# One more of eight depthwise-convolution channel blocks on the tensor engine, and another order of the layer norm's partial sums

## The chip, the cores and the metric

The kernel runs on one core of a Trainium2 chip. The metric is the device time of one execution in microseconds, as the median of several runs. Engines are called by their short names: PE is the tensor engine, DVE the vector engine, ACT ScalarE, POOL GpSimd, SP the engine that here only issues DMAs.

## The reference

Two decoder layers over 512 positions and 1024 channels, all in float32. Layer 0 mixes with an mLSTM, layer 1 with the convolution module below; each is followed by a gated MLP. The change lies in the convolution module alone:

```
C_KERNEL = 31

def conformer_conv_mixer(x, w_in, b_in, dw_w, dw_b, ln_g, ln_b, w_out, b_out):
    a = x @ w_in + b_in
    u = a[..., :D_MODEL] * jax.nn.sigmoid(a[..., D_MODEL:])
    u = causal_dwconv(u, dw_w, dw_b)
    u = jax.nn.silu(layernorm(u, ln_g, ln_b))
    return u @ w_out + b_out
```

The depthwise convolution has 31 taps for each channel. The layer norm takes mean and variance over all 1024 channels of a position.

## The kernel before, in words

Activations lie with channels on the 128 partitions and the 512 positions along the free axis, so 1024 channels are 8 blocks of 128 x 512. A matmul in float32 precision is made of three passes over operands that are split into a high and a low part (`mm3`): a weight unit of 128 x 1024 is loaded by SP, cast to its high part by ACT (line 151), and the rest is subtracted on DVE (line 152). Units come through rings: 4 raw, 3 high and 3 low. `next_unit` asks for the casts two units ahead.

The convolution stage runs over the 8 blocks j in order. `glu(j)` multiplies two weight units into two PSUM banks (24 matmuls for each unit), scales both on DVE, takes the sigmoid on ACT, and writes `u` on DVE. What then happens to `u` depends on the block's list:

- Blocks in `DVE_CH` and most taps of block 0 are convolved by taps on DVE: `dve_tap` (line 765), one fused multiply-add of 128 x 512 for each tap, into a PSUM bank.
- Block 1 (`POOL_CH`) and 13 taps of block 0 go by pairs: ACT makes the product of one tap (line 752, a ring of 4 buffers), POOL adds it (line 754). Block 0's two accumulators are joined later.
- Blocks in `PE_CH` go to PE. `shuffle` has ACT issue four DMAs that rearrange `u` into `us` (positions of four phases). `toeplitz` has POOL build block-diagonal weights `toe` of four groups (line 777). `conv_pe` multiplies them in two halves (line 804); each half is copied out by ACT (line 809) and goes back into channel order through two DMAs, one issued by ACT and one by SP (line 812). `us`, `toe` and the result each have a ring of two.

Taps wait in two lists, and `background(nv, ng)` takes so many from each. `PLAN` says what follows block j's own work: key 5 and 6 for the convolutions of blocks 3 and 5, key 14 and 15 (j + 8) for sums behind those of blocks 6 and 7.

`shift` takes the first PE block (`FIRST`), computes its mean over the 128 channels with a pair of matmuls (`col_mean`, lines 229 and 230, operands `ch` by ACT and `cl` by DVE), and uses this, `kb`, as an offset for all blocks. `stats(j, e)` subtracts it, squares on ACT, and adds block and square to `s1` and `s2` on engine e (POOL or DVE). The last PE block and the last DVE block are not added there; they go to the sums as parts of their own. `row_sums` (line 242) multiplies 128 x 128 pieces by two columns of 1/1024, and line 912 forms the mean over channels in all partitions. `warm(n, p)` runs n small float32 matmuls (two passes each, line 101) whose result nobody reads. Behind the sums come variance, a power on POOL, the broadcast of its rows, and for each block normalisation, activation and split on DVE and ACT, which feed the output projection (`out_proj`).

The order on each engine is made by a scheduler at build time: among the instructions that its own model holds ready, it takes the one that comes first in the program. `tc.issue_after(x)` holds an instruction behind x on its engine. On the chip each engine then works in that order.

Of the kernel before, what the change touches and what calls it, by code (L numbers as in the profile page):

```python
# [45 lines left out]
def hybrid_trunk(ctx, tc, x_in, par_in, tph_in, wg_in, wv_in, wqk_in, wo_in, mout_in, cin_in,  # L46
                 cout_in, up_in, down_in, out):
    nc = tc.nc
    V, A, G, PE = nc.vector, nc.scalar, nc.gpsimd, nc.tensor
# [12 lines left out]
    def nm(s):  # L62
        uid[0] += 1
        return f"{s}_{uid[0]}"

    def bank():
        return psum.tile([P, T], F32, tag="mm", name=nm("mm"))

    def small():
        return psms.tile([P, T], F32, tag="ms", name=nm("ms"))  # L70
# [5 lines left out]
    def pcol(name, i):  # L76
        o = _COLS[name] + i
        return par[:, o : o + 1]
# [8 lines left out]
    invd = const.tile([P, P], F32, name="invd")  # L87
# [8 lines left out]
    def warm(n, after=None):  # L96

        ps = bank()
        for _ in range(n):
            with tc.issue_after(after.ins) if after is not None else nullcontext():  # L100
                after = PE.matmul(ps[:, :P], ones, ones, start=True, stop=True)  # L101
# [8 lines left out]
    for what in "q0 o0 o1 q1 o2 o3 q2 o4 q3 o5 o6 o7".split():  # L110
        i = int(what[1])
# [25 lines left out]
    def feed_to(ndma, nsplit):  # L137
        while st["dma"] < min(ndma, len(seq)):
            i = st["dma"]
            ap, n = seq[i]  # L140
            r = wraw.tile([P, 1024], F32, tag="wr", name=f"wr{i}")
            nc.sync.dma_start(out=r[:, :n], in_=ap)
            raws[i] = r
            st["dma"] += 1
        while st["split"] < min(nsplit, len(seq)):
            i = st["split"]
            n = seq[i][1]
            r = raws.pop(i)
            hi = wsp.tile([P, 1024], F32R, tag="wh", name=f"wh{i}")
            lo = wsp.tile([P, 1024], F32R, tag="wl", name=f"wl{i}")  # L150
            st["last"] = A.copy(hi[:, :n], r[:, :n])  # L151
            V.tensor_tensor(out=lo[:, :n], in0=r[:, :n], in1=hi[:, :n], op=ALU.subtract)  # L152
            splits[i] = (hi, lo)
            st["split"] += 1
# [82 lines left out]
    def row_sums(ps, t, c, w, start, stop):  # L237

        nb = (c.stop - c.start) // P
        for b in range(nb):  # L240
            s = slice(c.start + b * P, c.start + (b + 1) * P)
            PE.matmul(ps[:, 2 * b : 2 * b + 2], t[:, s], w[:, :2], start=start and b == 0,  # L242
                      stop=stop and b == nb - 1)
# [458 lines left out]
    cctx = ExitStack()  # L702
    cp = cctx.enter_context(tc.tile_pool(name="conv", bufs=1))
    SPLIT = 0
    DVE_CH, POOL_CH, PE_CH = (0, 2, 4), (1,), (3, 5, 6, 7)
    NV, NG, NG4, NPRE = 4, 4, 13, 1
    cacc2 = cp.tile([P, T], F32, name="caccp")
    p128 = cp.tile([P, P], F32, name="p128")
# [8 lines left out]
    d = {}  # L717
# [77 lines left out]
    def conv_pe(j, us, toe):  # L795
        cacc[j] = cp.tile([P, T], F32, tag="cpe", name=f"cacc{j}", bufs=2)
        back = cacc[j].rearrange("p (q t) -> p q t", q=NPH)
        feed_to(st["get"] + 4, st["get"] + 3)
        front = st["last"] if j != PE_CH[1] else st["kb"]
        for hf in range(2):  # L800
            ps = bank()
            for g in range(2):
                for i in range(NJ):
                    p = PE.matmul(ps[:, g * NTAU : (g + 1) * NTAU], toe[:, 2 * hf + g, i, :],  # L804
                                  us[:, 2 * hf + g, NJ - 1 - i : NJ - 1 - i + NTAU],
                                  start=i == 0, stop=i == NJ - 1)
            co = cp.tile([P, 2, NTAU], F32, tag="co", name=nm("co"), bufs=4)
            with tc.issue_after(front.ins):
                A.copy(co.rearrange("p g t -> p (g t)"), ps[:, : 2 * NTAU])
            for g in range(2):  # L810
                o = 32 * (2 * hf + g)
                (nc.scalar if g == 0 else nc.sync).dma_start(out=back[o : o + 32], in_=co[:, g])
        return p
# [4 lines left out]
    def background(nv, ng):  # L818
        for q, n, f in ((vtaps, nv, dve_tap), (gtaps, ng, pool_tap)):
            for _ in range(min(n, len(q))):  # L820
                f(*q.pop(0))

    kb = cp.tile([P, T], F32, name="kb")
    s1 = cp.tile([P, T], F32, name="s1")
    s2 = cp.tile([P, T], F32, name="s2")

    FIRST, LAST = PE_CH[0], PE_CH[-1]
# [14 lines left out]
    def stats(j, e):  # L842
        if j in PE_CH:
            d[j] = cp.tile([P, T], F32, name=f"d{j}")
            V.scalar_tensor_tensor(
                out=d[j].rearrange("p (t q) -> p t q", q=NPH),
                in0=cacc[j].rearrange("p (q t) -> p t q", q=NPH), scalar=pcol("dw_b", j),
                in1=kb.rearrange("p (t q) -> p t q", q=NPH), op0=ALU.add, op1=ALU.subtract)
        elif j == SPLIT:
            d[j] = cacc[j]  # L850
            G.tensor_tensor(out=cacc2, in0=cacc2, in1=kb, op=ALU.subtract)
            V.tensor_tensor(out=d[j], in0=cacc[j], in1=cacc2, op=ALU.add)
        elif j == DVE_CH[-1]:
            d[j] = cacc[j]
            V.tensor_tensor(out=d[j], in0=pacc[j], in1=kb, op=ALU.subtract)
        else:
            d[j] = cacc[j]
            (e or V).tensor_tensor(out=d[j], in0=cacc[j], in1=kb, op=ALU.subtract)
        sq = cp.tile([P, T], F32, tag="csq", name=nm("csq"), bufs=2)
        A.activation(sq, d[j], AF.Square)  # L860
        if e is not None:
            e.tensor_tensor(out=s1, in0=s1, in1=d[j], op=ALU.add)
            e.tensor_tensor(out=s2, in0=s2, in1=sq, op=ALU.add)
        return sq

    PLAN = {
        5: [lambda: conv_pe(3, *us[3]), lambda: background(2 * NV, 0)],
        6: [shift, lambda: conv_pe(5, *us[5]), lambda: background(2 * NV, 0)],
        14: [lambda: stats(1, G), lambda: stats(5, V), lambda: stats(0, G)],
        15: [lambda: stats(2, V), lambda: stats(6, V)],  # L870
    }
    us = {}
    for j in range(8):
# [16 lines left out]
        with tc.issue_after(st["glu"].ins) if j == LAST else nullcontext():  # L890
            background(NV, NG)
            for f in PLAN.get(j, ()):
                f()
    for j in PE_CH[2:]:
        with tc.issue_after(st["glu"].ins):
            background(2 * NV, 2 * NG)
        p = conv_pe(j, *us[j])
        with tc.issue_after(st["glu"].ins), tc.issue_after(st["toe"].ins):
            for f in PLAN.get(j + 8, ()):
                f()  # L900
    warm(8, p)
    background(999, 999)
    sq7 = stats(LAST, None)
    sq4 = stats(DVE_CH[-1], None)


    pr1, pr2, pmu = small(), small(), bank()
    parts = ((s1, s2), (d[LAST], sq7), (d[DVE_CH[-1]], sq4))
    for i, (t1, t2) in enumerate(parts):
        row_sums(pr1, t1, slice(0, T), invd, i == 0, i == 2)  # L910
        row_sums(pr2, t2, slice(0, T), invd, i == 0, i == 2)
        p = PE.matmul(pmu, invd, t1, start=i == 0, stop=i == 2)  # L912
    warm(4, p)
    vm = work.tile([P, 3, NTB], F32, tag="vm", name="vm")
    V.tensor_copy(vm[:, 0], pr1[:, 0:8:2])
    V.tensor_tensor(out=vm[:, 1], in0=vm[:, 0], in1=vm[:, 0], op=ALU.mult)
# [101 lines left out]
```

## Time and profile before

| | us |
|---|---|
| median of 3 runs | 1158.98 |
| lowest, highest | 1155.64, 1160.68 |
| the profiled execution | 1161.23 |
| its span, from the first to the last instruction | 1159.5 |

All times within the kernel are counted from the start of the span. Mean granted clock of PE over the span: 0.985, where 1 is 2.4 GHz and 0.5 is 1.2 GHz. The convolution stage with its layer norm lies between about 596 and 741 us, and the second MLP follows it to the end.

### The profile page before, as it was taken

To read this page: it belongs to the slowest core of one execution; us is meant where nothing else is said; L and a number is where in the kernel's file an instruction comes from. 1 tells how busy PE (TensorE), PEld (TensorE's weight loads), DVE (VectorE), ACT (ScalarE), POOL (GpSimd) and SP (SyncE) were. 2 spreads that over 40 slices of the span, in tenths; PEclk is the share of its full clock that TensorE was granted. 3 is DMA by queue.
4 is the path that set the end of the run, shared out by engine and by line. 5 is a ranking of instruction groups with operands and counts; after the bars stand their busy time and mean duration, and the time that the engine had idled before them with its cause. 6 is when DMAs were issued, how large, how long until landed. Compare 5 with 4: busy or idle time off the path is not lost.

```text
span 1159.5 us, 13543 instructions
## 1 busy us (share of the span) xinstructions
PE 1134.3 (98%) x5262; PEld 944.4 (81%) x5262; DVE 746.7 (64%) x1013; ACT 512.2 (44%) x716; POOL 170.6 (15%) x132
## 2 busy tenths in 40 slices
PE   9999999999999999999989889999999999999996
PEld 7788888888888888888877779888888888888886
DVE  6688885477777777322367997565877777752222
ACT  6567774354444444322245542453444444432221
POOL 4000001100000000000049985020000000000002
PEclk9999999999999999999999999799999999999998
DMA  6232122232332332333222322032332322333312
GB/s 246 85 105 73 55 73 87 80 108 90 103 98 90 102 99 83 99 100 92 100 94 73 100 82 74 1 109 91 101 100 91 99 101 91 93 94 100 94 57 73
DMA packets 36369, 106.85 MB, mean 92 GB/s; under 512 B 4049, under 2 KB 10321, under 8 KB 36305
## 3 DMA queue, kind: packets, MB, share of 16 engines
q1 hardware_dynamic: 31728, 103.25, 27.8%
q10 hardware_dynamic: 4576, 2.74, 0.9%
q8 instruction: 41, 0.67, 0.2%
q14 instruction: 24, 0.19, 0.0%
HBM read 101.78 MB, written 2.10 MB: 90 GB/s over the span
## 4 chain that ended last, share of the span: by engine, by line
PE 88%; POOL 5%; DVE 4%; issue 1%; ACT 1%; DMA 0%; POOLq 0%; SPq 0%; ACTq 0%; DVEq 0%
PE mm L163 26%; PE mm L164 26%; PE mm L165 26%; PE mm L804 2%; PE mm L584 2%; PE mm L588 2%; PE mm L585 2%; POOL cacc L754 2%; POOL toe L777 2%; POOL caccp L754 1%; DVE mm L765 1%; PE ms L242 1%; DVE wl L152 1%; PE mm L101 0%; PE mm L912 0%
## 5 line engine op out<-in xcount | busy, mean ns | idle before, releaser
L163 PE MATMUL mm<-xh,wh 128*128 128x512 f32 x960 | 375.0, 391 | 4.3 <-ACT wh L151 2.7
L165 PE MATMUL mm<-xh,wl 128*128 128x512 f32 x960 | 374.9, 391 | 1.9 <-DVE wl L152 1.9
L164 PE MATMUL mm<-xl,wh 128*128 128x512 f32 x960 | 374.8, 390 | 0.0
L152 DVE TENSOR_TENSOR wl<-wr,wh 128x1024 fp32r<-128x1024 f32 (+1 forms) x192 | 240.1, 1253 | 167.3 <-ACT wh L151 165.2
L151 ACT CAST wh<-wr 128x1024 fp32r<-128x1024 f32 (+1 forms) x192 | 197.6, 1031 | 287.4 <-PE mm L164 237.1
L163 PEld LDWEIGHTS mm<-xh,wh 128*128 128x128 f32 x960 | 181.0, 189 | 42.6 <-ACT wh L151 3.6
L165 PEld LDWEIGHTS mm<-xh,wl 128*128 128x128 f32 x960 | 180.9, 188 | 40.5 <-DVE wl L152 2.7
L164 PEld LDWEIGHTS mm<-xl,wh 128*128 128x128 f32 x960 | 180.8, 188 | 37.5
L195 POOL TENSOR_TENSOR acc<-acc,sq 128x512 f32<-128x512 f32 x30 | 43.2, 1441 | 741.5 <-ACT sq L193 741.0
L164 PE MATMUL mm<-yl,wh 128*128 128x512 f32 (+1 forms) x374 | 140.9, 377 | 0.0
L163 PE MATMUL mm<-yh,wh 128*128 128x512 f32 (+1 forms) x374 | 140.9, 377 | 0.0
L165 PE MATMUL mm<-yh,wl 128*128 128x512 f32 (+1 forms) x374 | 140.8, 376 | 0.0
L614 DVE TENSOR_TENSOR mm<-mm,rsb 128x512 f32<-128x512 f32 x88 | 60.9, 696 | 76.0 <-PE mm L165 73.1
L163 PEld LDWEIGHTS mm<-yh,wh 128*128 128x128 f32 x374 | 70.4, 188 | 12.9
L165 PEld LDWEIGHTS mm<-yh,wl 128*128 128x128 f32 x374 | 70.4, 188 | 12.9
L164 PEld LDWEIGHTS mm<-yl,wh 128*128 128x128 f32 x374 | 70.4, 188 | 12.8
L624 ACT CAST yh<-ta 128x512 fp32r<-128x512 f32 x44 | 27.3, 620 | 104.6 <-DVE ta L623 104.6
L619 DVE SCALAR_TENSOR_TENSOR ta<-mm,par,ta 128x511 f32<-128x511 f32 x88 | 65.6, 746 | 1.3
L619 DVE SCALAR_TENSOR_TENSOR tb<-mm,par,tb 128x511 f32<-128x511 f32 x88 | 65.5, 746 | 1.4
L622 ACT ACTIVATE ta<-ta 128x512 f32<-128x512 f32 x44 | 27.8, 632 | 79.4 <-DVE ta L619 79.4
L765 DVE SCALAR_TENSOR_TENSOR mm<-u,par,mm 128x497 f32<-128x497 f32 (+14 forms) x76 | 55.8, 734 | 1.7
L625 DVE TENSOR_TENSOR yl<-ta,yh 128x512 fp32r<-128x512 f32 x44 | 30.4, 691 | 26.1 <-ACT yh L624 26.1
(245 smaller groups left out, 1230.3 us busy)
## 6 DMA issues: line engine op xcount, KB each, us to landing
wr<-in_dram SPq DMA_DIRECT2D x175, 512.0 KB, 3.5
wr<-in_dram SPq DMA_DIRECT2D x16, 384.0 KB, 3.2
xall<-in_dram SPq DMA_DIRECT2D x8, 256.0 KB, 6.2
us<-u ACTq DMA_DIRECT2D x16, 64.0 KB, 2.5
out_dram<-xall SPq DMA_DIRECT2D x2, 384.0 KB, 3.5
tph<-in_dram SPq DMA_DIRECT2D x1, 576.0 KB, 4.3
wr<-in_dram SPq DMA_DIRECT2D x2, 256.0 KB, 4.1
cacc<-co SPq DMA_DIRECT2D x8, 64.0 KB, 2.2
```

The lines of the kernel that those rows point to most:

```text
L151: st["last"] = A.copy(hi[:, :n], r[:, :n])
L152: V.tensor_tensor(out=lo[:, :n], in0=r[:, :n], in1=hi[:, :n], op=ALU.subtract)
L163: PE.matmul(ps, lh, rh, start=start, stop=False)
L164: PE.matmul(ps, lh, rl, start=False, stop=False)
L165: PE.matmul(ps, ll, rh, start=False, stop=stop)
L195: e.tensor_tensor(out=nrm.acc[:, c], in0=nrm.acc[:, c], in1=sq[:, c], op=ALU.add)
L614: V.tensor_tensor(out=ps, in0=ps, in1=rs["b"], op=ALU.mult)
L619: V.scalar_tensor_tensor(out=t[:, s:], in0=ps[:, : T - s], scalar=pcol("fconv_w", m * 3 + 2 - s), in1=t[:, s:], op0=ALU.mult, op1=ALU.add)
L622: A.activation(ta, ta, AF.Silu)
L625: V.tensor_tensor(out=yl[:, j, :], in0=ta, in1=yh[:, j, :], op=ALU.subtract)
L754: G.tensor_tensor(out=a[:, s:], in0=a[:, s:], in1=p[:, s:], op=ALU.add)
L765: V.scalar_tensor_tensor(out=a[:, s:], in0=u[:, : T - s], scalar=dw(j, CK - 1 - s), in1=a[:, s:], op0=ALU.mult, op1=ALU.add)
```

## The change

Block 2 leaves `DVE_CH` for `PE_CH`, where it comes first. So it is now block 2 that gives the offset `kb`; block 3 becomes an ordinary PE block, whose sums are added by `stats(3, V)` in `PLAN[6]`, in place of `stats(2, V)` in `PLAN[15]`. Block 2's convolution on PE follows `glu(4)`, `shift` and block 3's follow `glu(5)`, block 5's follows `glu(6)`. Two calls that took eight more DVE taps each are gone from `PLAN`. The parts of the layer norm are summed in another order: block 4's first, then `s1` and `s2`, then the last PE block's, whose mean comes behind both of its row sums. The warming matmuls that followed the last convolution come behind the second part.

```
-    DVE_CH, POOL_CH, PE_CH = (0, 2, 4), (1,), (3, 5, 6, 7)
+    DVE_CH, POOL_CH, PE_CH = (0, 4), (1,), (2, 3, 5, 6, 7)
...
     PLAN = {
-        5: [lambda: conv_pe(3, *us[3]), lambda: background(2 * NV, 0)],
-        6: [shift, lambda: conv_pe(5, *us[5]), lambda: background(2 * NV, 0)],
+        4: [lambda: conv_pe(2, *us[2])],
+        5: [shift, lambda: conv_pe(3, *us[3])],
+        6: [lambda: conv_pe(5, *us[5]), lambda: stats(3, V)],
         14: [lambda: stats(1, G), lambda: stats(5, V), lambda: stats(0, G)],
-        15: [lambda: stats(2, V), lambda: stats(6, V)],
+        15: [lambda: stats(6, V)],
     }
...
-    for j in PE_CH[2:]:
+    for j in PE_CH[-2:]:
...
-    warm(8, p)
     background(999, 999)
+    sq4 = stats(DVE_CH[-1], None)
     sq7 = stats(LAST, None)
-    sq4 = stats(DVE_CH[-1], None)
...
     pr1, pr2, pmu = small(), small(), bank()
-    parts = ((s1, s2), (d[LAST], sq7), (d[DVE_CH[-1]], sq4))
+    parts = ((d[DVE_CH[-1]], sq4), (s1, s2), (d[LAST], sq7))
     for i, (t1, t2) in enumerate(parts):
+        if i < 2:
+            p = PE.matmul(pmu, invd, t1, start=i == 0, stop=False)
         row_sums(pr1, t1, slice(0, T), invd, i == 0, i == 2)
         row_sums(pr2, t2, slice(0, T), invd, i == 0, i == 2)
-        p = PE.matmul(pmu, invd, t1, start=i == 0, stop=i == 2)
-    warm(4, p)
+        if i == 1:
+            warm(8, p)
+    warm(4, PE.matmul(pmu, invd, d[LAST], start=False, stop=True))
```

## Rows read from the trace of the kernel before

**Rows 1.** The page, part 1: busy time, share and instructions of each engine.

```profile
PE 1134.3 (98%) x5262; PEld 944.4 (81%) x5262; DVE 746.7 (64%) x1013; ACT 512.2 (44%) x716; POOL 170.6 (15%) x132
```

**Rows 2.** Stretches of the convolution stage: busy us of PE, PEld, DVE, ACT, POOL, clock, DMA.

```profile
609.00:622.00 13.00, 13.00 (x59) 10.78 (x58) 10.79 (x13) 6.09 (x10) 12.61 (x8) 1.00 0.27 83
...
671.00:691.00 20.00, 18.01 (x101) 15.84 (x99) 19.61 (x24) 7.99 (x12) 17.17 (x11) 0.91 0.28 79
```

**Rows 3.** Chain that ended last, convolution stage and layer norm: start, us, what.

```profile
602.38 11.45 POOL toe L777 x5
...
681.20 1.87 DVE cl L228
...
719.84 1.79 PE mm L101 x16
721.62 1.68 PE ms L242 x16
723.31 0.96 PE mm L912 x2
...
730.79 3.22 PE ms L242 x16
...
737.95 3.41 PE mm L101 x16
```

**Rows 4.** Timeline of PE, 637 to 742: start, us, instruction, idle time before and releaser.

```profile
637.00 0.50 PE L163 MATMUL mm<-xh,wh 128*128 128x512 f32 x1 [1.31 <-ACT wh L151]
...
652.59 0.50 PE L163 MATMUL mm<-xh,wh 128*128 128x512 f32 x1 [1.40 <-ACT wh L151]
...
659.21 8.20 PE L804 MATMUL mm<-us,toe 128*128 128x128 f32 x72
...
669.04 0.50 PE L163 MATMUL mm<-xh,wh 128*128 128x512 f32 x1 [1.63 <-ACT sg L732]
...
681.16 0.50 PE L229 MATMUL ms<-ch,pdvr 128*128 128x512 f32 x1 [0.97 <-ACT ch L227]
...
683.12 0.50 PE L230 MATMUL ms<-cl,pdvr 128*128 128x512 f32 x1 [1.02 <-DVE cl L228]
...
741.02 1.06 PE L163 MATMUL mm<-zht,wh 128*128 128x512 f32 x2
```

**Rows 5.** Waits of PE, 636 to 656: us in total, times, longest.

```profile
PE mm L165 <- DVE wl L152: 1.9, 2, 1.1
```

**Rows 6.** Stretches behind the first and the last wait, columns as in rows 2.

```profile
639.00:643.00 4.00, 4.00 (x11) 3.17 (x12) 3.89 (x7) 2.41 (x4) 3.77 (x4) 0.57 0.38 131
683.00:687.00 4.00, 3.88 (x20) 3.84 (x21) 3.96 (x5) 0.00 (x1) 4.00 (x2) 0.60 0.00 0
```

**Rows 7.** Who waited for POOL's additions (line 754): us, times.

```profile
  ACT cprod L752: 20.5, 19
```

**Rows 8.** Timeline of ACT, 619 to 677, columns as in rows 4.

```profile
619.96 1.04 ACT L151 CAST wh<-wr 128x1024 fp32r<-128x1024 f32 x1
...
666.78 1.03 ACT L151 CAST wh<-wr 128x1024 fp32r<-128x1024 f32 x1
...
672.35 3.00 ACTq L792 DMA_DIRECT2D us<-u  x4
...
676.17 0.37 ACT L809 COPY co<-mm 128x256 f32<-128x256 f32 x1
```

**Rows 9.** What PE waited for before the row sums (line 242): us, times.

```profile
  DVE d L845: 0.7, 1
```

**Rows 10.** Two stretches of the row sums, columns as in rows 2.

```profile
724.00:726.00 2.00, 2.00 (x10) 1.68 (x10) 0.07 (x1) 1.88 (x3) 0.00 (x0) 0.68 0.00 0
...
730.00:734.00 4.00, 4.00 (x18) 3.48 (x17) 0.00 (x0) 0.00 (x0) 0.00 (x0) 0.50 0.00 0
```

**Rows 11.** DVE's taps (line 765): ns of one, min/median/max, first and last start.

```profile
L765 DVE SCALAR_TENSOR_TENSOR mm<-u,par,mm x76: 712/734/758, 601.0 to 714.0; 128x497 f32<-128x497 f32 x3, 128x496 f32<-128x496 f32 x3, 128x495 f32<-128x495 f32 x3, 128x494 f32<-128x494 f32 x3
```

**Rows 12.** Timeline of POOL: the third weight build, columns as in rows 4.

```profile
676.22 8.82 POOL L777 TENSOR_TENSOR toe<-msk,tph 128x1152 f32<-128x1152 f32 x4
```

## The prediction, made before the changed kernel ran

> **What bounds the kernel now.** First the page's busy shares, which say where not to look: the tensor engine (PE) is busy 98% of the span, the vector engine (DVE) 64%, GpSimd (POOL) 15% [rows 1]. Work added to PE is added to the time, unless it stands where PE waits. Second the table by stretches of the convolution stage [rows 2]: PE is full at 609 to 622 us, but busy only 18.01 of 20 us at 671 to 691, where DVE is busy 19.61 and POOL 17.17. Here three engines are close to full, which the 98% doesn't say. Third the chain of waits [rows 3]. From 602 on it runs on POOL (building the block-diagonal weights "toe", then adding taps), later over ACT and DVE to the operand of a column mean at 681, and only then is PE itself the chain.
>
> Fourth, what PE waits for, in its timeline and waits [rows 4, 5]: 1.31 us at 637 and 1.40 at 652.6 for a weight cast on ScalarE (ACT), 1.9 in two for the subtraction on DVE that follows each cast (the longer, 1.1, after the first, so 0.8 after the second), 1.63 at 669 for a PSUM bank that ACT's sigmoid releases, 0.97 and 1.02 at 681 to 683 for the column mean; together 8.2 us. After the first and after the last of these the granted clock falls to its lower level: 0.57 and 0.60 over 4 us each [rows 6], which loses 0.43 x 4 = 1.7 us and 0.40 x 4 = 1.6 us.
>
> Why are weights late? ACT works in order, and between the casts stand the products for POOL's taps, which wait for POOL's buffers: 20.5 us in 19 waits [rows 7]. Eight casts, the first at 619.96, the last at 666.78 [rows 8], are 46.8 / 7 = 6.7 us apart; PE needs 24 matmuls of 13.00 / 59 us = 5.3 us a unit [rows 2]. So POOL sets the pace through ACT, and three buffers of lead are used up at 637.
>
> Last the tail. Block 7's convolution ends where the warming matmuls begin, at 719.84; call it C. Layer norm's row sums end at 730.79 + 3.22 = 734.0 = C + 14.2 [rows 3], and the output projection starts at 741.0 [rows 4]. For the last block's part, written late by DVE, PE idles 0.7 us in all [rows 9]: the sums are PE-bound, and the granted clock, 0.68 over 724 to 726, is 0.50 over 730 to 734 [rows 10].
>
> **Block 2 moves to PE.** It adds 72 matmul instructions. One convolution stands alone in PE's timeline: 8.20 us [rows 4]. Term: **+8.2 us**.
>
> It takes 30 taps x 0.734 = 22 us from DVE [rows 11]. I credit this with nothing by itself: DVE's subtractions only follow late casts, and at the column mean PE waits for ACT's cast first (to 681.16), DVE's part starting at 681.20, in the same moment [rows 3, 4]. What the move gives is worked out wait by wait:
> - 637 to 639 (2.4 us and 1.7 of clock): before any change on PE, and set by ACT behind POOL. Stays. Block 2's four DMA issues on ACT (3.00 us for four [rows 8]) come in ahead of that cast; the products there wait for POOL anyway, so I charge nothing, at most the 3.0 us.
> - 652 to 654 (2.2 us): block 2's convolution now stands before the unit ahead of it, so PE arrives 8.2 us later, at about 659; the cast was there at 652.6. Goes: **-2.2**.
> - 669 (1.63 us): one accumulator bank fewer is held, and PE comes later. Goes: **-1.6**.
> - 681 to 683 (2.0 us and 1.6 of clock): the same chain (copy out, DMA back, bias, cast, column mean) now starts from block 2 and stands before block 3's convolution, two units behind it, as now. In the profile the second copy out came at 676.17, with four DMA issues ahead of it from 672.35 to 675.35 [rows 8]; these go, but now ACT is among the paced products. Bounds: nothing left (-3.6), or 5 us instead of 2 (+3.0). I take -0.5, near the old row.
>
> Sum at C: 8.2 - 2.2 - 1.6 - 0.5 = **+3.9 us**, bounds +0.8 and, with +3.0 twice, +10.4.
>
> A fifth weight tile costs POOL 8.82 us [rows 12]. It is covered as long as it stands where the third tile stood before, which began only at 676.22. There it would end near 685, and PE reaches block 5's convolution at 683 + 4 or later. Without cover see the first rival. The fifth block's two SP copies stand in SP's queue ahead of weight loads, which are four units ahead; nothing. Removed calls that pull DVE's taps ahead, and block 3's two sums on DVE instead of block 2's: covered by the 22 us freed.
>
> **The order of the sums.** Before and after, PE does 48 row-sum matmuls, 6 of 512 columns and 16 warming ones behind C, and it was PE, not the late block, that set the end. Reordering alone thus saves nothing; block 4's part, ready early, could run before C only where PE waits, and there it hardly does. What changes is the clock. At the upper level 16 row sums take 1.68 us, a pair of wide ones 0.96, the 16 warming ones 1.79; at the lower 16 row sums take 3.22 and the 16 warming ones 3.41 [rows 3], a pair of wide ones twice 0.96 = 1.92. In the profile the clock fell once the first part's matmuls were through (721.62 to 724.27 [rows 3], then 0.68). I put the fall there again: block 4's part 2.64 us at the upper level, the sums' part 5.14 at the lower, the warming 3.4, the last part 2.64 if the warming lifts the clock, 5.14 if not. The sums end at C + 13.8 or C + 16.3, against C + 14.2. With the clock lifted, the second warming group shrinks too, from 3.41 to 1.79; I take 1.0 of these 1.6, as the projection's operands come close behind. Term: 13.8 - 14.2 - 1.0 = **-1.4 us**, bounds +2.1 and -5.5 (upper level throughout: 48 / 16 x 1.68 + 3 x 0.96 + 1.79 = C + 9.7, and -1.0).
>
> Total +3.9 - 1.4 = +2.5 us. The profiled execution took 1161.23 us, 2.25 above the median 1158.98 and 0.6 above the slowest of the three runs; on the profiled one that is 1163.7, on the median **1161.5**. A measurement of this kernel can tell about 0.5% (5.8 us) from no change, so this is no measurable change.
>
> **The rivals.**
> 1. POOL's fifth weight tile lands among the taps (slower). It may be built once block 2's convolution has freed its buffer, near 655, and in a gap of ACT's products POOL may take it at once. Then every product, copy and cast behind it on ACT is 8.8 us later, some 3 us of which PE had in hand at the column mean: 2.5 + 5.8 = +8.3, 1167.3. For it: POOL paces ACT until 667. Against: before, the third tile came only at 676 [rows 12]. It decides if the tile starts before about 667.
> 2. DVE's relief takes all of PE's waits away (faster). 8.2 - 8.2 - 3.3 = -3.3 at C, with the tail -4.7 to -8.8: 1152.2 in the middle. For it: DVE is busy 19.61 of 20 us at 671 to 691. Against: the first wait names ACT, and POOL behind it.
> 3. The tail at the full clock: 3.9 - 5.5 = -1.6, 1157.4. For it: the warming now stands between the sums and the last part, where PE might wait. Against: PE hardly waited before, and fell.
>
> The rows say that PE was busy 4.00 of 4.00 us from 730 to 734, at a granted clock of 0.50 [rows 10]. The Trainium skill, "TensorE: Matmul & The Clock Gate", section "HAM oscillation", puts a fallen clock down to idle gaps between matmuls; by that the third rival would be the likely one, since the new order leaves no gap. The rows don't agree: without a gap the clock stayed down.
>
> **How the numbers follow.** Forecast 0.50 (its own range 1157 to 1166, from the bounds at the column mean and the clock), rival 1 0.24, rival 2 0.14, rival 3 0.12. Slower by over 0.5% (above 1164.8): most of rival 1 and the forecast's upper edge, 0.24. Faster (below 1153.2): 0.10 of rival 2 and a little of rival 3, 0.12. Same: 0.64. The range leaves out about a tenth on each side: 1154 to 1168.5.
>
> **What would show it.** Right: 5 x 72 convolution matmuls, 46 instead of 76 taps on DVE; block 7's convolution ending about 4 us later than 719.84; the waits at 652 and 669 gone, that at 637 kept; the third weight build on POOL behind about 40 taps; from C to the projection's first matmul 19 to 21 us, with part of it at half clock. Wrong: PE waiting over 5 us before a convolution, for the column mean or for "toe"; no wait at 637, which would mean that ACT was held by DVE; or the sums ending before C + 11 or after C + 16.

## The result: 0.5% slower

| | before | changed |
|---|---|---|
| median, us | 1157.65 (7 runs) | 1164.59 (7 runs) |
| lowest, highest | 1155.64, 1160.84 | 1162.19, 1165.34 |
| the profiled execution | 1161.23 | 1164.59 |
| its span; mean granted clock | 1159.5; 0.985 | 1162.9; 0.990 |

The ratio is 1.0052, interval 1.0037 to 1.0067: 6.9 us more on the medians, where 2.5 were forecast. That is on the border between "no measurable change" and "slower by over 0.5%", and the interval lies on both sides of it.

The profiled execution of before took 3.6 us more than its median. So the stage is compared by the two profiles, and for the layer norm's tail it is kept in mind that [rows 3, 10] show a long one. From PE's first matmul of the stage (line 220) to the end of the last convolution the two profiles give:

| us from the start of the span | before | changed |
|---|---|---|
| stage begins | 595.30 | 596.57 |
| last convolution ends (C), by PE's own timeline | 719.67 | 728.11 |
| **stage** | 719.67 - 595.30 = **124.4** | 728.11 - 596.57 = **131.5** |
| first matmul of the projection | 741.02 | 744.66 |
| **tail** | 741.02 - 719.67 = **21.4** | 744.66 - 728.11 = **16.6** |

The stage is 7.1 us longer. The stage began 1.3 us later in this execution, ahead of anything that the change touches. If the typical tail of before is taken as 21.4 - 3.6 = 17.8 (an estimate, which puts all of that execution's excess into its tail), the tail gained 1.2. Together 7.1 + 1.3 - 1.2 = 7.2, beside 6.9 measured. So the loss is in the convolution stage.

**The profile after.** Part 1 of the page, beside [rows 1]; then what PE waited for between 598 and 740 us, beside [rows 4, 5]:

```profile
PE 1135.8 (98%) x5334; PEld 947.6 (81%) x5334; DVE 729.2 (63%) x982; ACT 513.2 (44%) x717; POOL 181.5 (16%) x137
```

```profile
PE ms L229 <- ACT ch L227: 8.1, 1, 8.1
PE ms L230 <- DVE cl L228: 1.9, 1, 1.9
```

PE has 5334 - 5262 = 72 more instructions, as expected, and shows the same 98%. The 8.2 us of waits before, in four places, are 10.0 us after, in one: the column mean. PE's timeline there and at the convolution that was added, beside [rows 4]:

```profile
642.44 8.20 PE L804 MATMUL mm<-us,toe 128*128 128x128 f32 x72
...
669.72 0.79 PE L229 MATMUL ms<-ch,pdvr 128*128 128x512 f32 x1 [8.15 <-ACT ch L227]
...
672.37 0.79 PE L230 MATMUL ms<-cl,pdvr 128*128 128x512 f32 x1 [1.86 <-DVE cl L228]
```

PE came to the column mean at 669.72 - 8.15 = 661.6. The chain of waits, beside [rows 3], and ACT's timeline, beside [rows 8], say why its operand was not there:

```profile
664.80 0.36 ACT co L809
665.18 2.49 DMA cacc<-co
...
667.84 1.19 ACT d L832
669.05 0.63 ACT ch L227
669.70 2.63 DVE cl L228
672.37 0.79 PE ms L230
```

```profile
660.23 0.71 ACT L752 ACTIVATE cprod<-u,par 128x492 f32<-128x492 f32 x1 [0.64 <-POOL cacc L754]
660.85 0.35 ACT L809 COPY co<-mm 128x256 f32<-128x256 f32 x1
...
664.19 0.70 ACT L752 ACTIVATE cprod<-u,par 128x489 f32<-128x489 f32 x1 [0.60 <-POOL cacc L754]
664.80 0.35 ACT L809 COPY co<-mm 128x256 f32<-128x256 f32 x1
```

Block 2's convolution was through on PE at 650.6, but ACT copied its halves out only at 660.85 and 664.80: in ACT's order products for POOL's taps stand ahead of the copies, and each of these waits for POOL to free a buffer. Then come the way back (2.5 us of DMA), the bias, the cast and DVE's part, 7.6 us from the second copy to PE's last matmul of the mean. The clock by stretches, beside [rows 6, 10]:

```profile
661.00:673.00 12.00, 1.99 (x6) 0.97 (x5) 10.27 (x13) 6.96 (x10) 11.77 (x9) 0.67 0.08 22
673.00:693.00 20.00, 20.00 (x121) 18.10 (x120) 14.82 (x16) 7.75 (x14) 19.07 (x13) 0.94 0.26 79
...
734.00:737.00 3.00, 3.00 (x18) 3.00 (x17) 0.00 (x0) 1.18 (x1) 0.00 (x0) 0.56 0.00 0
737.00:740.00 3.00, 3.00 (x22) 2.52 (x23) 1.00 (x5) 0.00 (x0) 0.86 (x1) 1.00 0.01 3
```

In the wait PE is busy 1.99 of 12 us and POOL 11.77. The clock fell mostly while PE had nothing to do; behind it 0.06 x 20 = 1.2 us were lost. Most of the stage in one stretch, before and then changed, columns as in [rows 2]:

```profile
598.00:715.00 117.00, 108.81 (x582) 92.99 (x582) 104.39 (x125) 56.90 (x84) 105.68 (x68) 0.97 0.26 78
598.00:715.00 117.00, 106.99 (x581) 92.48 (x581) 80.06 (x84) 57.05 (x82) 113.68 (x71) 0.95 0.26 77
```

DVE is relieved of 24 us. ACT is as busy as before, and POOL has 8 us more to do.

### The profile page after: what moved, and what is told of

Same layout as the page of the kernel before. It is cut to its first block, busy times and chain, and to the rows that moved or that the text cites. A ratio compares the mean times of both kernels' runs of the same rounds, so it can differ in the third digit from the quotient of the medians.

```text
span 1162.9 us, 13686 instructions
## 1 busy us (share of the span) xinstructions
PE 1135.8 (98%) x5334; PEld 947.6 (81%) x5334; DVE 729.2 (63%) x982; ACT 513.2 (44%) x717; POOL 181.5 (16%) x137
## 4 chain that ended last, share of the span: by engine, by line
PE 88%; POOL 5%; DVE 3%; issue 2%; ACT 1%; DMA 1%; POOLq 0%; SPq 0%; ACTq 0%
PE mm L163 26%; PE mm L164 26%; PE mm L165 26%; PE mm L804 3%; POOL cacc L754 2%; PE mm L588 2%; PE mm L585 2%; PE mm L584 2%; POOL toe L777 2%; POOL caccp L754 1%; DVE wl L152 1%; PE ms L242 0%; DMA xall<-in_dram 0%; ACT wh L151 0%; PE mm L101 0%
## 5 line engine op out<-in xcount | busy, mean ns | idle before, releaser
L622 ACT ACTIVATE ta<-ta 128x512 f32<-128x512 f32 x44 | 27.9, 633 | 79.1 <-DVE ta L619 79.1
L777 POOL TENSOR_TENSOR toe<-msk,tph 128x1152 f32<-128x1152 f32 x20 | 45.5, 2306 | 2.8 <-DVE msk L721 2.8
```

The costliest lines, as they stand in the source:

```text
L777: st["toe"] = G.tensor_tensor(out=toe[:, g].rearrange("p n (c q) -> p n c q", q=NPH), in0=msk4[:].unsqueeze(1).to_broadcast([P, NJ, b, NPH ...
```

## The experiments

The letters of the theories are those of the expectations. Stage, tail and waits are read from each profile as above (the stage from line 220 to C, the tail from C to the projection); waits are PE's in the stage. The kernel before ran again beside each group of experiments, and its median lay between 1155.90 and 1157.70; so a difference of a us or two between kernels of different groups (e1 to e4; e5 to e8; e9 to e11; e12) is not read.

| | median | ratio to before | stage | tail | waits |
|---|---|---|---|---|---|
| sums alone (e1) | 1154.00 | 0.9968 (0.9956 to 0.9979) | 124.1 | 14.9 | 8.6 in all |
| block 2 alone (e2) | 1168.97 | 1.0104 (1.0087 to 1.0122) | 131.6 | 22.5 | 8.1 + 1.8 |
| column mean later (e3) | 1167.12 | 1.0081 (1.0061 to 1.0102) | 133.5 | 20.3 | 3.6 + 6.4 |
| fifth tile on DVE (e4) | 1163.98 | 1.0061 (1.0046 to 1.0076) | 133.3 | 14.9 | 11.0 + 0.2 |
| 5 taps of block 0 on POOL (e5) | 1161.70 | 1.0037 (1.0023 to 1.0051) | 128.4 | 17.1 | 1.1 + 5.3 |
| e3 and e4 (e6) | 1163.92 | 1.0058 (1.0040 to 1.0075) | 128.8 | 20.3 | 6.0 + 1.1 |
| e1 with 5 taps (e7) | 1161.84 | 1.0033 (1.0017 to 1.0048) | 117.4 | 27.9 | 3.1, then 5.5 |
| sums, warming first (e8) | 1156.96 | 0.9999 (0.9986 to 1.0013) | 123.8 | 17.7 | 8.1 in all |
| no products (e9) | 1160.36 | 1.0027 (1.0012 to 1.0042) | 128.2 | 19.7 | 6.2 |
| e1, no products (e10) | 1146.76 | 0.9932 (0.9908 to 0.9955) | 116.2 | 14.9 | 3.9 |
| way back on DVE (e11) | 1164.88 | 1.0073 (1.0056 to 1.0091) | 134.1 | 15.5 | 1.2 + 8.2 + 1.7 |
| no products, squares behind (e12) | 1157.93 | 1.0000 (0.9987 to 1.0014) | 119.9 | 23.1 | 0 |

**The two halves of the change.** Only the new order of the sums, in the kernel before:

```diff
-    warm(8, p)
...
-    sq7 = stats(LAST, None)
     sq4 = stats(DVE_CH[-1], None)
+    sq7 = stats(LAST, None)
...
-    parts = ((s1, s2), (d[LAST], sq7), (d[DVE_CH[-1]], sq4))
+    parts = ((d[DVE_CH[-1]], sq4), (s1, s2), (d[LAST], sq7))
     for i, (t1, t2) in enumerate(parts):
+        if i < 2:
+            p = PE.matmul(pmu, invd, t1, start=i == 0, stop=False)
...
-        p = PE.matmul(pmu, invd, t1, start=i == 0, stop=i == 2)
-    warm(4, p)
+        if i == 1:
+            warm(8, p)
+    warm(4, PE.matmul(pmu, invd, d[LAST], start=False, stop=True))
```

> The kernel before with the new order of the sums alone (block 4's part first, warming matmuls behind the second part). Theory A (the new order is what shortened the stretch from the last convolution to the output projection from 21.2 to 16.4 us, by keeping the clock up): about 4 us faster than before, and 16 to 18 us in that stretch. Rival (the sums are bound by the tensor engine in either order, and the clock in that one execution was chance): within 1 us of before, 20 us or more in the stretch.

Only block 2's move, that is, the changed kernel with these lines taken back:

```diff
+    warm(8, p)
...
-    parts = ((d[DVE_CH[-1]], sq4), (s1, s2), (d[LAST], sq7))
+    parts = ((s1, s2), (d[LAST], sq7), (d[DVE_CH[-1]], sq4))
```

> The changed kernel with the old order of the sums. Theory A: the move of block 2 alone costs what the whole change costs plus what the sums give back, 7 + 4 = 11 us more than before. Rival: the sums give nothing, so it costs the same as the whole change, 7 us.

The sums alone gave 1157.70 - 1154.00 = 3.7 us; the move alone cost 1168.97 - 1157.70 = 11.3. They add up: 11.3 - 3.7 = 7.6, beside 6.9 for both. With the sums alone the granted clock stays up for the whole tail, where [rows 10] fell, and the nine runs lie within 0.7 us (1153.85 to 1154.53), where the fourteen of before beside them reach from 1155.69 to 1161.44. Two of the stretches:

```profile
721.00:724.00 3.00, 3.00 (x24) 2.52 (x23) 1.10 (x1) 0.29 (x1) 0.00 (x0) 1.00 0.16 44
724.00:727.00 3.00, 3.00 (x29) 3.00 (x29) 0.00 (x0) 1.62 (x2) 0.00 (x0) 1.00 0.00 0
```

**Where the warming matmuls stand.** e1, but `warm(8, p)` back behind the last convolution:

```diff
+    warm(8, p)
     background(999, 999)
...
-        if i == 1:
-            warm(8, p)
```

> The kernel before with the new order of the sums, but with the warming matmuls left right behind the last convolution. Theory A1 (what keeps the clock up is that the warming matmuls stand between the sums and the last part): the clock falls to its lower level within the sums as before, and the gain of 3.7 us goes, to within 1 us of before. Rival A2 (the order of the parts alone, with the wide matmuls ahead of their row sums, does it): 3 us or more faster than before, as with the whole of the new order.

1156.96, ratio 0.9999: the gain is gone. The tail is 17.7 us, and the clock falls again in the row sums. The stretches:

```profile
724.00:727.00 3.00, 3.00 (x24) 2.52 (x23) 1.10 (x1) 1.01 (x2) 0.00 (x0) 1.00 0.00 0
727.00:730.00 3.00, 3.00 (x19) 3.00 (x19) 0.00 (x0) 0.90 (x1) 0.00 (x0) 0.60 0.00 0
730.00:733.00 3.00, 3.00 (x11) 2.48 (x12) 0.66 (x4) 0.00 (x0) 0.61 (x1) 0.50 0.00 0
```

So what e1 gains lies in the warming group's place among the sums; the order of the parts by itself gives nothing. That place does not keep the clock up behind every stage: in e3, e6, e9 and e12 it fell all the same. PE is busy 3.00 of 3.00 us where the clock falls: as in the prediction, the rows do not bear out the Trainium skill ("TensorE: Matmul & The Clock Gate", section "HAM oscillation"), by which idle gaps between matmuls would be what lowers it.

**The fifth weight tile.** Taken off POOL, in the changed kernel:

```diff
-                st["toe"] = G.tensor_tensor(
+                st["toe"] = (V if j == 5 else G).tensor_tensor(
```

> The changed kernel with block 5's weight tile built by VectorE instead of GpSimd, which takes 8.8 us from GpSimd in the middle of the taps. Theory A: the copies out that the column mean waits for stand ahead of that tile on their way, so the wait stays at 8 to 10 us and the time within 2 us of the changed kernel. Rival B: the wait for the column mean shrinks by 6 us or more and the time falls by as much.

1163.98 against 1164.59: nothing. The wait at the column mean stays:

```profile
PE ms L229 <- ACT ch L227: 11.0, 1, 11.0
```

In the changed kernel that tile began at 665.48, by POOL's timeline, and the copy on which the chain runs at 664.80 (row above). The tile stood behind the chain, not in it.

```profile
665.48 8.82 POOL L777 TENSOR_TENSOR toe<-msk,tph 128x1152 f32<-128x1152 f32 x4
```

**The column mean later.** Behind `glu(6)` instead of `glu(5)`, so that two units more lie between block 2's convolution and its mean:

```diff
-        front = st["last"] if j != PE_CH[1] else st["kb"]
+        front = st["last"] if j != PE_CH[2] else st["kb"]
...
-        5: [shift, lambda: conv_pe(3, *us[3])],
-        6: [lambda: conv_pe(5, *us[5]), lambda: stats(3, V)],
+        5: [lambda: conv_pe(3, *us[3])],
+        6: [shift, lambda: conv_pe(5, *us[5]), lambda: stats(3, V)],
```

> The changed kernel with the column mean of block 2 moved from ahead of block 3's convolution to ahead of block 5's, two weight units and one convolution later. Theory A (the tensor engine waits 8.1 + 1.9 us for the column mean because ScalarE copies block 2 out late, behind products that GpSimd paces; the clock falls behind that wait): the wait shrinks to 2 us or less and the time falls by 8 to 13 us against the changed kernel, to 2 to 5 us below the kernel before. Rival B (GpSimd's fifth weight tile among the taps is what holds the stage): the tensor engine waits for the tile or for what stands behind it instead, and the time stays within 3 us of the changed kernel.

1167.12, no gain. The waits of PE:

```profile
PE mm L804 <- ACT co L809: 6.4, 1, 6.4
PE mm L163 <- ACT sg L732: 3.6, 1, 3.6
```

The wait at the column mean is gone, and 3.6 + 6.4 = 10.0 us stand elsewhere: at a bank that ACT's sigmoid releases, and ahead of block 7's convolution, at a bank that ACT copies out. Only the place moved. Ahead of the second wait ACT stands still for 6.24 us, at a square that waits for POOL; behind that square come the DMA issues for block 7's convolution. ACT's timeline:

```profile
710.91 0.63 ACT L860 ACTIVATE csq<-cacc 128x512 f32<-128x512 f32 x1 [6.24 <-POOL cacc L858]
```

Both edits together:

> The changed kernel with both edits that gained nothing one by one: the column mean ahead of block 5's convolution, and block 5's weight tile built by VectorE. Theory C: with 8.8 us off GpSimd and the first wait out of the way, the waits for a bank (3.6) and ahead of block 7's convolution (6.4) that came with the moved column mean fall to 2 us or less together, and the time falls by 6 to 10 us against the changed kernel. Rival D: these waits stay, and the time stays within 3 us of the changed kernel.

1163.92, 0.7 us below the changed kernel, which is no difference, as the rival had it. The waits shrink to 7.1, of which the sigmoid's is now 6.0. The stage is 131.5 - 128.8 = 2.7 us shorter, but the tail took 20.3.

**Less for POOL.** 5 instead of 13 taps of block 0 go the way over ACT and POOL, the other 8 to DVE; first in the changed kernel, then in e1:

```diff
-    NV, NG, NG4, NPRE = 4, 4, 13, 1
+    NV, NG, NG4, NPRE = 4, 4, 5, 1
```

> The changed kernel with 5 instead of 13 of block 0's taps on GpSimd, the other 8 on VectorE, which lies idle for most of 620 to 655 us in the changed kernel. Theory C (GpSimd's stream of 43 taps and 20 weight builds, with ScalarE's products tied to it, sets the length of the whole stage; removing one wait of the tensor engine only moves it): the copies out of block 2 come 8 x 1.45 = 11.6 us earlier, the wait for the column mean falls from 10 us to 2 or less, nothing takes its place, and the time falls by 8 to 13 us against the changed kernel. Rival D (what stands late in ScalarE's order, not the length of GpSimd's stream, makes the waits): as with the moved column mean another wait of 6 us or more appears, and the time stays within 3 us of the changed kernel.

> The kernel before with the new order of the sums and 5 instead of 13 of block 0's taps on GpSimd; block 2 stays on VectorE. Theory C: GpSimd's relief is worth something here only if VectorE, busy 19.6 of 20 us at 671 to 691, has room for 8 x 0.73 = 5.9 us more; the wait of 2 us for the column mean, which VectorE's taps stand beside, grows, and the time is 0 to 5 us above the order of the sums alone (1154). Rival D: the weight casts come earlier and the waits at 637 and 652 (4.6 us with 1.7 of clock) go, so the time falls by 3 us or more below 1154.

In the changed kernel 2.9 us were gained: 1161.70, the wait at the column mean 5.3 instead of 10.0. Neither theory was met in full: theory C had 8 to 13 us, theory D another wait of 6 us. The wait doesn't vanish, since the copies still stand behind a product that waits. ACT's timeline:

```profile
661.58 0.70 ACT L752 ACTIVATE cprod<-u,par 128x483 f32<-128x483 f32 x1 [0.62 <-POOL cacc L754]
662.19 0.35 ACT L809 COPY co<-mm 128x256 f32<-128x256 f32 x1
```

In e1 the same edit made the stage 124.1 - 117.4 = 6.7 us shorter, and the kernel 7.8 us slower (1161.84 against 1154.00): with three blocks and eight more taps DVE is late at the end, and the tail waits for block 4. Both theories missed this: C had at most 5 us more, and a longer wait at the column mean. A row of PE's timeline:

```profile
720.07 2.08 PE L910 MATMUL mm<-cacc,invd 128*128 128x512 f32 x2 [5.48 <-DVE cacc L855]
```

That 5.48 is part of a tail of 27.9, in which the clock was low too.

**ACT untied from POOL.** No products: POOL adds `u` itself, so the multiplication by these 43 tap weights is left out. In the changed kernel (e9) and in e1 (e10):

```diff
-        p = cp.tile([P, T], F32, tag="cprod", name=nm("cprod"), bufs=4)
-        A.mul(p[:, s:], u[:, : T - s], dw(j, CK - 1 - s))
         a = cacc2 if j == SPLIT else cacc[j]
-        G.tensor_tensor(out=a[:, s:], in0=a[:, s:], in1=p[:, s:], op=ALU.add)
+        G.tensor_tensor(out=a[:, s:], in0=a[:, s:], in1=u[:, : T - s], op=ALU.add)
```

> The changed kernel without ScalarE's products: GpSimd adds the shifted block itself, so the multiplication by those 43 tap weights is left out. GpSimd keeps its 43 additions and 20 weight builds; ScalarE no longer waits for GpSimd's four buffers. Theory D (the tensor engine waits because its casts, copies out and sigmoids stand in ScalarE's order between products that wait for GpSimd): the wait of 10 us for the column mean falls to 2 or less, no other of more than 3 us comes, and the time falls by 8 to 14 us against the changed kernel, to 1151 to 1157. Theory C (the length of GpSimd's own stream sets the stage): the stream is as long as before, and the time stays within 3 us of the changed kernel.

> The kernel before with the new order of the sums and without ScalarE's products, as in the run beside it: what the move of block 2 costs once ScalarE is not tied to GpSimd. Theory D: the waits for weights at 637 and 652 go, and the time is 1147 to 1151; the run beside it lies above it by at most the 8.2 us of one convolution. Rival (VectorE, not ScalarE, holds the kernel before): the waits go but others, behind VectorE's taps, take their place, and the time stays within 2 us of 1154.

e10 came out as theory D had it, a quarter of a us below its range: 1146.76, which is 7.2 us under e1. Two of its seven runs took 1151.71 and 1154.10, and by the ratios to before (0.9932 against 0.9968) the gain is about 4 us. The profiled execution has the stage at 116.2 and the waits at 3.9 in all, the longest three of them here:

```profile
PE ms L229 <- ACT ch L227: 1.4, 1, 1.4
PE mm L802 <- ACT co L807: 1.2, 1, 1.2
PE ms L230 <- DVE cl L228: 0.7, 1, 0.7
```

In e9 the wait at the column mean went too, as theory D had it, but the kernel gained only 4.2 us instead of 8 to 14, and lies 13.6 us above e10, where theory D had at most 8.2: another wait, of 6.2, stood ahead of block 7's convolution. ACT's timeline there:

```profile
704.94 0.63 ACT L858 ACTIVATE csq<-cacc 128x512 f32<-128x512 f32 x1 [10.02 <-POOL cacc L856]
...
709.50 2.60 ACTq L790 DMA_DIRECT2D us<-u  x4
712.19 0.37 ACT L807 COPY co<-mm 128x256 f32<-128x256 f32 x1 [5.10 <-DMA us<-u]
```

A square on ACT waits 10.02 us for POOL, which subtracts the offset from block 1 only behind the tile of block 7; behind that square, in ACT's order, stand the DMA issues that bring block 7's `us`. It is the second tie between ACT and POOL, the one that e3 had met too.

**That tie taken away too.** e9, with the squares of the sums in the loop held behind block 7's DMA issues:

```diff
-                nc.scalar.dma_start(out=us[:, g, NJ - 1 :], in_=up[32 * g : 32 * g + 32])
+                st["us"] = nc.scalar.dma_start(out=us[:, g, NJ - 1 :], in_=up[32 * g : 32 * g + 32])
...
-        with tc.issue_after(st["glu"].ins), tc.issue_after(st["toe"].ins):
+        with tc.issue_after(st["glu"].ins), tc.issue_after(st["toe"].ins), tc.issue_after(st["us"].ins):
```

> The changed kernel without ScalarE's products (the multiplication by 43 tap weights is left out, as before), and with ScalarE's squares for blocks 1, 5 and 0 held behind the DMAs that rearrange block 7. Without the products alone one wait of 6.2 us was left, ahead of block 7's convolution, where ScalarE stood waiting for GpSimd's last weight tile and the sum behind it. Theory E (these two, the products and that square, are all that the tensor engine waits for; with both gone the stage is bound by the tensor engine, and the fifth convolution costs its own length): the wait falls to 1 or less, the time is 1151 to 1155, and lies 5 to 8 us above the kernel before without products (1146.8). Rival: a further wait of 3 us or more takes its place, and the time stays above 1157.

PE waits for nothing in the stage any more, and the last two convolutions run in one piece, 16.54 us for 144 matmuls:

```profile
698.43 16.54 PE L802 MATMUL mm<-us,toe 128*128 128x128 f32 x144
```

The stage takes 119.9. Against e10, which lacks the move and this edit of the squares, that is 3.7 us more; the convolution's 8.2 less e10's 3.9 us of waits are 4.3. POOL is about as busy as in the changed kernel, 112.55 of 117 us, and PE 116.94:

```profile
598.00:715.00 117.00, 116.94 (x695) 103.31 (x695) 91.27 (x96) 29.73 (x42) 112.55 (x72) 1.00 0.29 84
```

The time, 1157.93, missed the 1151 to 1155 that theory E had, and the 5 to 8 us above e10 (it is 11.2). The loss lies outside the stage: the tail is 23.1, with the clock down from some 4 us behind C (714.83). Just ahead of that, at 717.66, PE waits 0.91 us for ACT's square of block 4, so the edit reaches into the tail; whether it brought the fall was not tested. The stretches:

```profile
718.00:721.00 3.00, 3.00 (x13) 1.97 (x12) 0.00 (x0) 0.37 (x1) 0.00 (x0) 0.60 0.34 92
721.00:724.00 3.00, 3.00 (x15) 3.00 (x15) 1.10 (x1) 0.93 (x2) 0.00 (x0) 0.50 0.00 1
724.00:727.00 3.00, 3.00 (x15) 3.00 (x15) 0.00 (x0) 0.99 (x1) 0.00 (x0) 0.50 0.00 0
```

**Block 2's way back taken off ACT.** e5, with block 2's copies, bias and cast on DVE and its DMAs issued by SP:

```diff
-                A.copy(co.rearrange("p g t -> p (g t)"), ps[:, : 2 * NTAU])
+                (V.tensor_copy if j == FIRST else A.copy)(co.rearrange("p g t -> p (g t)"), ps[:, : 2 * NTAU])
...
-                (nc.scalar if g == 0 else nc.sync).dma_start(out=back[o : o + 32], in_=co[:, g])
+                (nc.scalar if g == 0 and j != FIRST else nc.sync).dma_start(out=back[o : o + 32], in_=co[:, g])
...
-        A.activation(d[FIRST].rearrange("p (t q) -> p t q", q=NPH),
-                     cacc[FIRST].rearrange("p (q t) -> p t q", q=NPH), AF.Identity,
-                     bias=pcol("dw_b", FIRST))
+        V.tensor_scalar(out=d[FIRST].rearrange("p (t q) -> p t q", q=NPH),
+                        in0=cacc[FIRST].rearrange("p (q t) -> p t q", q=NPH),
+                        scalar1=pcol("dw_b", FIRST), scalar2=None, op0=ALU.add)
...
-        col_mean(pk, d[FIRST], slice(0, T), pdvr)
+        col_mean(pk, d[FIRST], slice(0, T), pdvr, V.tensor_copy)
```

> The changed kernel with 8 of block 0's taps on VectorE instead of GpSimd, and with block 2's way back (copies out, bias, cast) on VectorE and its DMAs on SP instead of ScalarE. Theory D: the wait of 5.3 us for the column mean that was left with the 8 taps moved falls to 2 or less, and the time from 1161.7 to 1154 to 1158. Rival: VectorE's own order, with block 4's taps ahead of the copies, is as late as ScalarE's; the wait stays at 4 us or more and the time within 2 us of 1161.7.

1164.88, which is 3.2 us above e5. The rival was right on the wait, 8.2 + 1.7 us; the time rose by more than the 2 us that it allowed. DVE has an order of its own, and its taps stand ahead of each copy. Its timeline:

```profile
654.70 3.90 DVE L765 SCALAR_TENSOR_TENSOR mm<-u,par,mm 128x510 f32<-128x510 f32 x5
658.50 0.42 DVE L809 COPY co<-mm 128x256 f32<-128x256 f32 x1
658.84 3.87 DVE L765 SCALAR_TENSOR_TENSOR mm<-u,par,mm 128x505 f32<-128x505 f32 x5
662.61 0.42 DVE L809 COPY co<-mm 128x256 f32<-128x256 f32 x1
...
665.93 1.61 DVE L832 TENSOR_SCALAR d<-cacc,par 128x512 f32<-128x512 f32 x1 [0.69 <-DMA cacc<-co]
```

## Why the prediction came out as it did

The direction and the size of the main term were right, the size of the sum was not: +2.5 us forecast, +6.9 measured.

- **Block 2 on PE, +8.2**: as forecast, 8.20 us (row above).
- **The waits at 652 and 669, -2.2 and -1.6**: gone, as forecast.
- **The wait at 637, "stays"**: failed. Before, seven products stand on ACT between the cast at 625.88 and the one at 635.91 that PE waited for. After, four of them stand between the casts at 627.13 and 634.09, with block 2's four DMA issues among them. Three products had gone behind the cast; the prediction charged those issues with 0 to 3 us and did not see that the order around them would change (what part of the move changed it was not tested). That is 2.4 us of wait and 1.7 of clock, -4.1, forecast as 0. The casts in ACT's timeline, before and then after:

```profile
625.88 1.03 ACT L151 CAST wh<-wr 128x1024 fp32r<-128x1024 f32 x1
...
635.91 1.03 ACT L151 CAST wh<-wr 128x1024 fp32r<-128x1024 f32 x1
```

```profile
627.13 1.03 ACT L151 CAST wh<-wr 128x1024 fp32r<-128x1024 f32 x1
...
634.09 1.05 ACT L151 CAST wh<-wr 128x1024 fp32r<-128x1024 f32 x1
```

- **The column mean, -0.5 (bounds -3.6 and +3.0)**: the step that failed. The wait there is 8.15 + 1.86 = 10.0 instead of 2.0: +8.0, beyond the bound of 5 us in all. The clock behind it lost 1.2 instead of 1.6. The prediction saw that ACT would be among the paced products there, but left the copies about as close behind the convolution as before. Before, the second copy came 676.17 - 667.41 = 8.8 us behind the end of the convolution, and PE stood at the mean 681.16 - 0.97 - 667.41 = 12.8 us behind it [rows 4, 8]. After, the copy came 664.80 - 650.64 = 14.2 us behind it, and PE 661.57 - 650.64 = 10.9. A copy 5.4 us later and a PE 1.9 us sooner make 7.3 of the 8.0. The saving at 637 went into this wait too: with those 4.1 us kept, PE would have come that much later, and the wait would have been about 5.9 (an estimate, if ACT's order stays).
- **The sum at C, +3.9 (bounds +0.8 and +10.4)**: 8.2 - 2.2 - 1.6 - 4.1 + 8.0 - 1.6 + 1.2 = +7.9, beside 131.5 - 124.4 = +7.1 between the profiles. 0.8 us stay open. That the time still lies within the stated 1154 to 1168.5 owes something to luck: the errors at 637 (-4.1) and at the mean (+7.6 with the clock, where -0.5 was forecast) have opposite signs, and +4.0 of them was left.
- **The sums, -1.4 (bounds -5.5 and +2.1)**: alone they give -3.7 (e1). The clock did not fall again where the prediction put it, and e8 shows that the place of the warming group is the reason. By profiles C to the projection takes 16.6, not the 19 to 21 that the prediction named.

Two of the signs that the prediction named for being wrong came: PE waits over 5 us for the column mean, and the wait at 637 is gone. The second was to mean that DVE had held ACT; the rows show fewer products ahead of the cast instead. Two of the signs for being right did not come: C is 8.4 us later instead of about 4, and POOL began the third weight build behind 33 taps instead of about 40.

**The rivals.** The first, POOL's fifth tile among the taps, had its condition met: it began at 665.48, ahead of 667. Its mechanism is refuted all the same: the chain to the column mean does not go through it, and e4, which takes it away, leaves the time alone. The second, DVE's relief, was half right: the waits went at three of the four places, but their time came back at the fourth, and that it was DVE's relief that took them away is not shown. The third, the tail at the full clock, is what e1 shows; in the changed kernel the clock fell once, for some 3 us.

**What sets the waits.** Shown: with ACT untied from POOL's taps the kernel with four PE blocks gains 4 to 7 us (e10), and the waits at the column mean go in the changed one too (e9); with the second tie gone PE waits for nothing (e12); with neither gone, moving the mean (e3), the tile (e4) or both (e6) leaves 7 to 11 us of waits and changes only where they stand. Theory C, that the length of POOL's own stream sets the stage, is refuted by e12: POOL is about as busy there, and PE waits for nothing. So PE's waits in this stage are set by ACT, working in order between products and squares that wait for POOL. The runs without products take away some 27 us of ACT's own work (57.05 - 30.03 in e9 over the same stretch) together with its waits for POOL, and the two were not separated; but ACT was busy only half of that stretch, 57.05 of 117 us, so that the waits are what counts is argued, not shown. The move adds 8.2 us to an engine that is full, and gives no relief to the two engines that make it wait.

**What stays open.** In e3, e6, e9 and e12 the tail took 20 to 23 us with the clock low, in e1, e4, e10 and e11 14.9 to 15.5, with the same order of the sums. What tells them apart was not found; so part of what a shorter stage gives is lost behind it in some kernels, and their medians are not read for the stage alone. Nor is a profiled tail always the usual one: e3's profiled execution took 1168.91 us, where its runs reach from 1163.21 to 1169.47, and e9's, 1163.47, was the longest of its twelve.

The version that beats both kernels is e1: four PE blocks as before, and the new order of the sums: 1154.00, ratio 0.9968 (0.9956 to 0.9979).

## What to carry to other kernels

When an engine that is 98% busy waits a little in several places for one that works in order and is paced by a third, removing some of those waits only brings it to the next place sooner: add up all the waits that the same pacer causes, and ask where they will stand next; here they came to 7 to 11 us wherever the mean and the tile were moved. Before work is moved to the full engine, ask whether the engine that is relieved is the one it waits for; here it was DVE that was relieved, while ACT and POOL set the pace. A queue order made at build time can shift when instructions are added to that queue, as it did at 637, so a wait that "stays" is worth a range, not a point.

## What was unexpected of the hardware

The granted clock fell to its lower level while PE was busy in every microsecond: in e8 it is 1.00 over 724 to 727, then 0.60 and 0.50 over 727 to 733 (busy 9.00 of 9.00). In e12 it stayed at 0.50 over 721 to 727 (busy 6.00 of 6.00). The order of e12's instructions behind C kept 1.00 in e1. Moving 16 small matmuls from right behind C to 5 us later (724.30 in e1, with C at 719.09), between the row sums, was worth 3.0 us (e8 against e1), beside the 6.9 that the whole change cost.
